# A rotary-embedding kernel: the cos and sin tables move from ScalarE's DMA queue to SyncE's

## The chip, the cores and the metric

The kernel runs on one core of one Trainium2 chip. The metric is the device time of one execution in microseconds. Before the change the median of three runs is 162.42 us (162.38 to 162.75).

## The reference

The input `x` has 16 batches of 512 positions of 1024 numbers (16 heads of 64). Each head is split into two halves of 32, and the halves are rotated by the angle of their position, whose cosine and sine stand in two tables of 512 x 32:

```python
def reference(x, cos, sin, num_heads):
    x = x.reshape(batch, seq, num_heads, head_dim)
    x1, x2 = x[..., :half_dim], x[..., half_dim:]
    cos = cos[None, :, None, :]
    sin = sin[None, :, None, :]
    return np.concatenate([x1 * cos - x2 * sin, x1 * sin + x2 * cos], axis=-1)
```

All of it is float32. 33.55 MB are read as `x` and 33.55 MB are written; the two tables have 64 KB each.

## The kernel before

**Tiles.** `x` is cut into 8 tiles of two batches. A tile has 128 partitions (2 batches x 64), and each partition holds 8 consecutive positions ("rows" below, of 1024 numbers, so 4 KB) in one piece of 32 KB. A whole tile is 4 MB. Five buffers in SBUF (`bufs`, L73) hold tiles; tiles 5, 6 and 7 use the buffers of tiles 0, 1 and 2 again.

**Loads and stores.** `load` (L78 to L80) and `store` (L82 to L84) issue DMAs on SyncE, so on SyncE's queue, in the order of the program, which the kernel fixes by hand (`manual_schedule`, L65). The first tile is loaded in four pieces, rows 0, 1, 2 to 3 and 4 to 7 (L86 and L90), the second in two, the others whole. After the loads of tiles 0 to 4 come the stores of tiles 0 to 2, the loads of tiles 5 to 7, the stores of tiles 3 and 4, and then those of tiles 5 to 7, the last in three pieces. A load into a used buffer waits for the store that emptied it, and a store waits for the compute of its tile. Each DMA counts its completion on one of eight semaphores, taken in turn in the order of the program over both queues; a DMA that takes a semaphore again waits for the one that had it before. So the whole loads of tiles 2, 3 and 4 (the ninth to eleventh DMA) wait for the first three DMAs, which are row 0 of tile 0 and the two tables.

**Tables.** The two tables go to the tile `tabs` (L87), 64 partitions of 1 KB each, by two DMAs that ScalarE issues on a queue of its own (L88 sin, L89 cos). GpSimd meanwhile builds an identity and from it a selection matrix `sel` (L95 to L104). TensorE multiplies each table by `sel` (L111), which copies the 64 partitions to 128: sin first, into the PSUM tile `pp`, then cos into `tab`. ScalarE makes from the sine a table `sns` in SBUF that has both signs (L116, L117), and a small one for two rows in PSUM, in the tile `tab`.

**Compute.** A tile's rows are worked in groups of two or three (GROUPS, L41), by a plan written out by hand for each tile (PLAN, L42). T is the product of the swapped halves with the signed sine on GpSimd (L144); B is the same on VectorE (also L144); P is the product with the cosine on VectorE, into PSUM (L147); S is the sum of the two on VectorE, back into the tile (L149). For some groups the sum goes another way: A is the cosine product in place on VectorE (L151), and M adds by two matmuls with the identity into PSUM (L156, L158), which ScalarE copies back (L159). In the first tile the plan begins with T and P of group 3, which has rows 0 and 1. So the first piece of GpSimd's work waits for rows 0 and 1 and for `sns`; the first of VectorE's waits for those rows and for the cosine in `tab`, and its second, the sum, for GpSimd's first product.

Of the kernel before, what the change touches and what calls it, by code (L numbers as in the profile page):

```python
# [12 lines left out]
def kernel(  # L13
# [8 lines left out]
    nc = tc.nc  # L22
# [32 lines left out]
    cosv = cos.rearrange("(p r) j -> p (r j)", r=R)  # L55
    sinv = sin.rearrange("(p r) j -> p (r j)", r=R)
# [21 lines left out]
    def load(t, *cuts):  # L78
        for a, b in cuts or ((0, R),):
            loads[t].append(nc.sync.dma_start(out=x_tiles[t][:, a * dim:b * dim], in_=xv[t][:, a * dim:b * dim]))  # L80
# [4 lines left out]

    load(0, (0, 1))  # L86
    tabs = fixed.tile([HP, 2, R * half], FP32, name="tabs")  # L87
    nc.scalar.dma_start(out=tabs[:, 1], in_=sinv)  # L88
    nc.scalar.dma_start(out=tabs[:, 0], in_=cosv)  # L89
    load(0, (1, 2), (2, 4), (4, 8))  # L90
    load(1, (0, 3), (3, 8))
    for t in range(2, NB):
# [5 lines left out]
        out=ident, in_=ident, compare_op=ALU.not_equal, fill=1.0,  # L98
# [5 lines left out]
                          in_=bass.AP(tensor=i64.tensor, offset=i64.offset, ap=[i64.ap[0], [0, BP], [1, HP]]))  # L104
# [117 lines left out]
```

## Time and profile before

| what | before |
|---|---|
| median of three runs | 162.42 us (162.38 to 162.75) |
| the profiled execution | 162.55 us |
| its span, first to last instruction | 160.8 us |
| VectorE (DVE) busy | 138.4 us, 86% of the span |
| GpSimd (POOL) busy | 130.3 us, 81% |
| TensorE (PE) busy | 58.5 us, 36% |
| ScalarE (ACT) busy | 14.1 us, 9% |
| moved by DMA | 67.25 MB, mean 418 GB/s over the span |

The profile is that of one execution. "Busy" counts an engine's compute instructions; instructions that only issue a DMA are not counted, and the views mark them with a q behind the engine's name (SPq for SyncE, ACTq for ScalarE). q1 is SyncE's DMA queue and q10 ScalarE's. A DMA is spread over 16 DMA engines. The share of a queue is the time that its packets took, as a share of these 16 engines' time in the stretch that is looked at. "To landing" is the time from the issue of a DMA until its completion has been counted. A packet's whole time is put down where it begins, so that shares of short stretches may be above 1.

### The profile page before, as it was taken

How to read it: one execution, taken by the hardware profiler on the slowest of the kernel's cores; microseconds unless marked ns; L12 is line 12 of the kernel's file. 1: busy time of each engine (PE TensorE's matmuls, PEld its weight loads, DVE VectorE, ACT ScalarE, POOL GpSimd, SP SyncE). 2: the span in 40 equal slices, each digit the busy share in tenths (PEclk: the TensorE clock that was granted, in tenths of full speed). 3: DMA queues.
4: the chain of work that ended last, by engine and by line, in shares of the span. 5: the costliest groups of instructions: out<-in, count | busy, mean ns of one | idle time of the engine just before them, and what ended most of it. 6: DMA issues, size and time to landing. Idle time of an engine off the chain costs nothing.

```text
span 160.8 us, 394 instructions
## 1 busy us (share of the span) xinstructions
PE 58.5 (36%) x84; PEld 18.3 (11%) x84; DVE 138.4 (86%) x48; ACT 14.1 (9%) x25; POOL 130.3 (81%) x29
## 2 busy tenths in 40 slices
PE   0500000130488803088702378896868620000000
PEld 0200000100122100032101022222222200000000
DVE  0069999999999999999999999999998999999300
ACT  3200000000011110011200011102121210000000
POOL 2299999999979299995999199999999999992000
PEclk9999999999999995557995555559999995555555
DMA  5999999999999999999999999999999999999994
GB/s 164 384 450 417 460 432 465 391 432 481 391 391 505 399 399 489 416 399 481 424 399 448 457 399 432 473 391 432 473 399 424 467 408 416 465 424 408 404 441 199
DMA packets 3329, 67.25 MB, mean 418 GB/s; under 512 B 384, under 2 KB 512, under 8 KB 768
## 3 DMA queue, kind: packets, MB, share of 16 engines
q1 hardware_dynamic: 3168, 67.11, 97.8%
q10 hardware_dynamic: 160, 0.13, 0.2%
q14 instruction: 1, 0.01, 0.0%
HBM read 33.69 MB, written 33.55 MB: 418 GB/s over the span
## 4 chain that ended last, share of the span: by engine, by line
DVE 37%; POOL 27%; DMA 18%; PE 7%; issue 2%; ACT 2%; DVEq 0%; POOLq 0%
POOL T L144 27%; DVE x_sb L149 18%; DVE pp L147 16%; DMA x_sb<-in_x_dram 16%; PE ps L158 3%; PE ps L156 3%; DMA tabs<-in_sin_dram 3%; DVE x_sb L151 1%; DVE T L144 1%; ACT x_sb L159 1%; PE pp L111 1%; ACT sns L116 0%; ACT sns L117 0%; DVEq L149 0%; POOLq L144 0%
## 5 line engine op out<-in xcount | busy, mean ns | idle before, releaser
L144 POOL TENSOR_TENSOR T<-x_sb,sns 128x3072 f32<-128x3072 f32 (+1 forms) x22 | 129.3, 5927 | 14.7 <-ACT sns L117 5.4
L147 DVE TENSOR_TENSOR pp<-x_sb,tab 128x3072 f32<-128x3072 f32 (+1 forms) x20 | 60.8, 3040 | 8.8 <-ACT tab L117 8.3
L149 DVE TENSOR_TENSOR x_sb<-T,pp 128x3072 f32<-128x3072 f32 (+1 forms) x20 | 60.7, 3033 | 2.9 <-POOL T L144 1.5
L156 PE MATMUL ps<-T,ident 128*128 128x512 f32 x40 | 30.5, 854 | 47.1 <-POOL T L144 27.7
L158 PE MATMUL ps<-x_sb,ident 128*128 128x512 f32 x40 | 28.6, 807 | 18.9 <-DVE x_sb L151 18.9
L159 ACT COPY x_sb<-ps 128x512 f32<-128x512 f32 x20 | 11.7, 586 | 110.4 <-PE ps L158 110.4
L156 PEld LDWEIGHTS ps<-T,ident 128*128 128x128 f32 x40 | 7.6, 237 | 69.8 <-POOL T L144 29.2
L158 PEld LDWEIGHTS ps<-x_sb,ident 128*128 128x128 f32 x40 | 9.7, 252 | 34.8 <-DVE x_sb L151 23.3
L151 DVE TENSOR_TENSOR x_sb<-x_sb,tab 128x2048 f32<-128x2048 f32 x5 | 11.4, 2281 | 0.0
L144 DVE TENSOR_TENSOR T<-x_sb,tab 128x2048 f32<-128x2048 f32 x3 | 6.8, 2280 | 0.0
L111 PE MATMUL pp<-tabs,sel 64*128 64x256 f32 x2 | 1.2, 697 | 5.1 <-DMA tabs<-in_sin_dram 5.1
L116 ACT ACT_TABLE_LOAD x1 | 1.3, 1283 | 1.9 <-issue 1.9
L111 PE MATMUL tab<-tabs,sel 64*128 64x256 f32 x2 | 1.2, 708 | 0.3 <-DMA tabs<-in_cos_dram 0.3
L111 PEld LDWEIGHTS pp<-tabs,sel 64*128 64x128 f32 x2 | 0.5, 310 | 5.0 <-issue 5.0
L116 ACT COPY sns<-pp 128x256 f32<-128x256 f32 x1 | 0.4, 373 | 3.1 <-PE pp L111 3.1
L111 PEld LDWEIGHTS tab<-tabs,sel 64*128 64x128 f32 x2 | 0.5, 310 | 1.0 <-DMA tabs<-in_cos_dram 1.0
L96 POOL MEMSET ident<- 128x128 f32 x1 | 0.2, 205 | 0.3 <-POOLq L203 0.3
L117 ACT ACTIVATE sns<-pp 128x256 f32<-128x256 f32 x1 | 0.4, 390 | 0.0
L97 POOL TENSOR_SCALAR_AFFINE_SELECT ident<-ident 128x128 f32<-128x128 f32 x1 | 0.3, 292 | 0.1
L103 POOL COPY sel<-ident 64x128 f32<-64x128 f32 x1 | 0.3, 283 | 0.1
L203 POOL MEMSET const-float32-0.0<- 128x1 f32 x1 | 0.1, 98 | 0.2 <-issue 0.2
L116 ACT COPY tab<-pp 128x64 f32<-128x64 f32 x1 | 0.2, 197 | 0.9 <-PE tab L111 0.9
(4 smaller groups left out, 0.5 us busy)
## 6 DMA issues: line engine op xcount, KB each, us to landing
out_dram<-x_sb SPq DMA_DIRECT2D x7, 4096.0 KB, 20.8
x_sb<-in_x_dram SPq DMA_DIRECT2D x6, 4096.0 KB, 29.1
out_dram<-x_sb SPq DMA_DIRECT2D x2, 1536.0 KB, 12.6
x_sb<-in_x_dram SPq DMA_DIRECT2D x1, 2560.0 KB, 20.4
x_sb<-in_x_dram SPq DMA_DIRECT2D x1, 2048.0 KB, 11.7
x_sb<-in_x_dram SPq DMA_DIRECT2D x1, 1536.0 KB, 14.8
x_sb<-in_x_dram SPq DMA_DIRECT2D x2, 512.0 KB, 4.5
x_sb<-in_x_dram SPq DMA_DIRECT2D x1, 1024.0 KB, 7.3
```

What stands on the lines that cost most here:

```text
L97: nc.gpsimd.affine_select(out=ident, in_=ident, compare_op=ALU.not_equal, fill=1.0, base=0, pattern=[[-1, P]], channel_multiplier=1,)
L103: nc.gpsimd.tensor_copy(out=sel.rearrange("k (b p) -> k b p", b=BP), in_=bass.AP(tensor=i64.tensor, offset=i64.offset, ap=[i64.ap[0], [0, ...
L111: spread = [nc.tensor.matmul(out=o.rearrange("p r j -> p (r j)"), lhsT=sel, rhs=tabs[:, i], start=True, stop=True) for i, o in ((1, sin_ps ...
L116: signed.append(nc.scalar.copy(out=o[:, :, 1, :], in_=sin_ps[:, r0:r0 + o.shape[1], :]))
L117: signed.append(nc.scalar.mul(out=o[:, :, 0, :], in_=sin_ps[:, r0:r0 + o.shape[1], :], mul=-1.0))
L144: return [eng.tensor_tensor(out=Ts[t, k], in0=swapped(xr, n), in1=tb, op=ALU.mult)]
L147: return [nc.vector.tensor_tensor(out=pps[t, k], in0=xr, in1=cosb(k), op=ALU.mult)]
L149: return [nc.vector.tensor_tensor(out=xr, in0=Ts[t, k], in1=pps[t, k], op=ALU.add)]
L151: return [nc.vector.tensor_tensor(out=xr, in0=xr, in1=cosb(k), op=ALU.mult)]
L156: made.append(nc.tensor.matmul(out=ps, lhsT=ident, rhs=Ts[t, k][:, c * C:(c + 1) * C], start=True, stop=False))
L158: made.append(nc.tensor.matmul(out=ps, lhsT=ident, rhs=xc, start=False, stop=True))
L159: made.append(nc.scalar.copy(out=xc, in_=ps))
```

## The change

Both table DMAs are issued by SyncE in place of ScalarE. They stand where they stood in the program: behind the load of row 0 of the first tile and ahead of that of row 1. Nothing else in the kernel's text is different.

```diff
     load(0, (0, 1))
     tabs = fixed.tile([HP, 2, R * half], FP32, name="tabs")
-    nc.scalar.dma_start(out=tabs[:, 1], in_=sinv)
-    nc.scalar.dma_start(out=tabs[:, 0], in_=cosv)
+    nc.sync.dma_start(out=tabs[:, 1], in_=sinv)
+    nc.sync.dma_start(out=tabs[:, 0], in_=cosv)
     load(0, (1, 2), (2, 4), (4, 8))
     load(1, (0, 3), (3, 8))
     for t in range(2, NB):
```

In the built kernel ScalarE's instructions begin with its table load in place of the two DMAs, and SyncE's second and third DMA are now the two tables. VectorE, GpSimd and TensorE have the same instructions in the same order; their waits name other semaphores of the same DMAs (row 0 and sin have changed places in the row of semaphores).

## Prediction

> **What bounds the kernel now.** I first read the page's slices and its DMA queues, because the busiest engine (VectorE, 86%) leaves 14% of the span open.
>
> ```profile
> DVE  0069999999999999999999999999998999999300
> ...
> DMA  5999999999999999999999999999999999999994
> ...
> q1 hardware_dynamic: 3168, 67.11, 97.8%
> q10 hardware_dynamic: 160, 0.13, 0.2%
> ```
>
> The DMA row is full from the second slice to the last but one, while VectorE's (DVE) begins a slice later and ends two slices earlier; nearly all of it is SyncE's queue, q1. I then asked for the same by stretches; the last two columns are the share of the 16 DMA engines and GB/s.
>
> ```profile
> 0.00:3.00 3.00, 0.00 (x0) 0.00 (x0) 0.00 (x0) 1.05 (x1) 0.98 (x7) 1.00 0.39 81
> 3.00:8.00 5.00, 2.40 (x4) 1.00 (x4) 0.00 (x0) 1.05 (x4) 0.96 (x1) 1.00 1.03 388
> 8.00:140.00 132.00, 56.08 (x80) 17.31 (x80) 128.54 (x45) 11.97 (x22) 122.65 (x22) 0.83 1.01 433
> 140.00:158.00 18.00, 0.00 (x0) 0.00 (x0) 9.81 (x4) 0.00 (x0) 5.66 (x1) 0.50 0.99 424
> 158.00:161.00 3.00, 0.00 (x0) 0.00 (x0) 0.00 (x0) 0.00 (x0) 0.00 (x0) 0.50 0.23 98
> ```
>
> From 3 to 158 us the DMA engines are never idle and move 66.71 MB at 430 GB/s (the DMA view of that stretch). So the time is a sum: about 3 us of start-up, 155 us of a full DMA queue, 2.8 us to the span's end, and 1.75 us outside the span (162.55 - 160.8).
>
> Has compute slack everywhere? A DMA lands when the queue reaches it, so the question is whether each store is issued before the queue has run empty. The DMA view, over the moment of each issue, gives the time to landing. The store of tile 0 is issued at 30.06 and lands 32.8 later, at 62.9; that of tile 1 is issued at 56.82, 6.0 us before. The store of tile 2 (66.12) comes 6.5 us before that of tile 1 lands (56.82 + 15.8). The last store is issued at 150.09 with 9.9 us to landing, although its 1.5 MB take only 3.7 us at 430 GB/s. Taking off some 1.7 us, the worst of what lies between the last bytes and a landing and between an issue and its first bytes, about 4 us of slack are left at the tightest place. The page's chain of waits names VectorE (37%) and GpSimd (27%) and begins with the sin table, but it ends at VectorE's last sum at 150.05: it passes over the queue in which the last store stands. I take the DMA queue as the bound, and the chain as a path with 4 us to spare.
>
> **The start, step by step.** The timeline of the first 12 us (start, duration, what, and in brackets the idle time before):
>
> ```profile
> 0.73 0.53 ACTq L88 DMA_DIRECT2D tabs<-in_sin_dram  x1
> 0.74 6.15 SPq L80 DMA_DIRECT2D x_sb<-in_x_dram  x9
> ...
> 1.30 0.62 ACTq L89 DMA_DIRECT2D tabs<-in_cos_dram  x1
> ...
> 5.07 1.19 PE L111 MATMUL pp<-tabs,sel 64*128 64x256 f32 x2 [5.07 <-DMA tabs<-in_sin_dram]
> 6.29 0.37 ACT L116 COPY sns<-pp 128x256 f32<-128x256 f32 x1 [3.07 <-PE pp L111]
> ...
> 6.58 1.22 PE L111 MATMUL tab<-tabs,sel 64*128 64x256 f32 x2 [0.33 <-DMA tabs<-in_cos_dram]
> 7.04 8.97 POOL L144 TENSOR_TENSOR T<-x_sb,sns 128x2048 f32<-128x2048 f32 x2 [5.39 <-ACT sns L117]
> ...
> 8.31 2.30 DVE L147 TENSOR_TENSOR pp<-x_sb,tab 128x2048 f32<-128x2048 f32 x1 [8.31 <-ACT tab L117]
> 11.57 2.29 DVE L149 TENSOR_TENSOR x_sb<-T,pp 128x2048 f32<-128x2048 f32 x1 [0.97 <-POOL T L144]
> ```
>
> In windows of 0.2 us SyncE's queue has its first packets from 1.7; ScalarE's has none until 3.5, though sin was issued at 0.73. In longer windows q10 has 80 packets from 3.4 to 4.2, none from 4.2 to 5.1 and 80 from 5.1 to 5.9, while q1's 80 in the middle window are 4 KB each. So the order on the DMA engines is row 0, sin, row 1, cos, rows 2 and 3: sin is already directly behind row 0, and only cos changes places with row 1. A table costs the 16 engines 24.1% of 0.8 us = 0.19 us (cos 25.4%, 0.20).
>
> (The Trainium skill, DMA: Bandwidth & Descriptors, "Queues, rings and completion order", says that each DMA engine takes turns between the queues that have work, a packet of typically 9 to 17 descriptors at a time. A DMA of 128 partitions gives each engine 8 pieces, so the order above agrees. By this rule alone the change does no more than swap cos and row 1.)
>
> **Part by part.**
> 1. *Removed from ScalarE*: two issues, 0.53 + 0.62 = 1.15 us. ScalarE's table load (1.28 us at 1.95) comes earlier, but ScalarE then waits 3 us for TensorE. Worth 0.
> 2. *Added to SyncE*: two issues between those of row 0 (0.74) and row 1 (1.17). Each is bounded by SyncE's shortest issue at L80, 0.33, and ScalarE's longer one, 0.62; I take 0.45, the middle of the steps between SyncE's first issues (0.43 to 0.59). Row 1 is issued at about 2.1 (1.8 to 2.4), and five issues behind it move by the same 0.9. Cover: row 0's issue took 1.0 us to its first packets (0.74 to 1.7), so row 1's are there at 3.1 (2.8 to 3.4). The queue works on row 0 until about 3.6 and then on two tables, 0.39, to 4.0. Cover to spare: 0.6 to 1.2. Without cover the whole 0.9 would be paid, since the DMA queue is the bound. Later loads are farther ahead: the whole load of tile 4 (SyncE's last issue of the start, at 6.56) lands 46.6 us after it. Cost 0.
> 3. *Moved on the DMA engines*: the same bytes in the same packets, in one queue. From nothing in the total: 0. Row 1, now behind cos, lands 0.2 later, at 6.5 (1.17 + 5.2 = 6.4 before). Its first reader is GpSimd at 7.04, which waited for `sns`, ready at 6.95. Cost 0, with 0.4 to spare.
> 4. *Cos earlier*: it lands about 0.2 behind sin (4.9), at 5.1 in place of 6.5. Its matmul then follows that of sin at 6.27 in place of 6.58, and VectorE's first product starts at about 8.0 in place of 8.31. Next in line is GpSimd: VectorE's sum at 11.57 waits for GpSimd's product that started at 7.04 and ends at 11.55. So the 0.3 us turn into a longer wait there (0.97 to about 1.3). Gain 0.
> 5. *Sin*: still directly behind row 0; it lands at 4.9, as before, give or take 0.1.
> 6. *Semaphore waits*: the whole loads of tiles 2, 3 and 4 wait for the same three DMAs as before (row 0, sin, cos). The last may be issued at about 5.5 in place of 6.56; it stands behind the loads before it either way. 0.
>
> Sum: 0 on the profiled 162.55, and 0 on the median; I predict **162.4**. Unknown are two ends. Below: bytes moved until 3.0 are 0.24 MB (the DMA view of 0 to 3), 0.56 us of a full queue, while 1.3 us had passed since the first packets at 1.7; at most 0.7 us are to be had from a better ramp. Above: a table that leaves the queue empty costs up to the 0.64 us by which row 0's first packets trailed its issue (end of issue about 1.1, packets at 1.7).
>
> (The same page, "Issuing engines are not separate DMA queues", says that issuing from several engines saves only the sequencer's issue time. That speaks against the change: by it SyncE gives back the 0.9 us of step 2, and the sum would be 163.3 if they were exposed. The windows above put 0.6 us and more of transfer over them, so I hold them to be hidden.)
>
> **Rivals.**
> - *Slower: small DMAs in one queue run it dry.* Place: between row 0 and row 1. If the engines fetch a queue's next DMA only when the last is nearly drained, a table that lasts 0.2 us doesn't cover the 0.64 us that a start takes, and the queue idles 0.45 us for each: 2 x 0.45 = +0.9, so 163.3. It decides from a start that takes over 0.4 us with nothing ahead. For: today two queues alternate here, so that one can prepare while the other runs; and q10's packets came 2.2 us after their issue. Against: large pieces in q1 follow each other with no gap (share 1.03 from 3 to 8 us). 16%.
> - *Faster: a quicker ramp.* Between 2.1 and 2.3 no packet starts, 0.4 us after the first ones, just when ScalarE's issues are being worked on. If they hold up row 0, the change gives 0.4 to 0.7 us, so 162.0 to 161.7. Against: the first reads after a start may need this time alone. 16%.
> - *The chain of compute decides after all.* Then the end follows GpSimd's first product. By steps 3 and 5 that moves by -0.1 to +0.1, so 162.3 to 162.5: the same forecast, by another reason. 5%.
> - That the tables don't move is excluded: SyncE's built instructions have them second and third.
>
> **Numbers.** About 0.3% (0.49 us) is what a measurement of this kernel can tell from no change: 161.9 to 162.9 is "same". Forecast 63%, rival slower 16%, rival faster 16%, chain 5%. Faster by over 0.3%: 0.11 from the ramp (some two thirds of 0.4 to 0.7 lie past 0.49) and 0.03 for parts that add up, 0.14. Slower: 0.16 of the rival and 0.02 for step 2's cover failing, 0.18. Same: 0.68. The range takes in the ramp's whole 0.7 below (161.7) and one of the two empty stretches with some more above (163.0).
>
> **What would show it.** Right: one queue, q1, with 3328 packets; no packet-free stretch between 3 and 158; cos's matmul at about 6.3, VectorE's first product at 8.0 and its wait before 11.6 grown to 1.3; GpSimd's first at 7.0. Wrong: a share well under 1 between 3.4 and 4.5, or row 1 landing after 7.0 (slower rival), row 0 landing well before 4.6 (faster rival), or the last landing moving with GpSimd's first start (chain).

## The result, and the profile after

The changed kernel is slower: a median of 164.68 us (163.70 to 165.63, six executions) against 162.58 us (162.38 to 163.11, six) for the kernel before on the same chip, a ratio of 1.0124 with a 95% interval of 1.0104 to 1.0144. The forecast was 162.4 and "no change". The profiled execution of the changed kernel took 163.70 us, the fastest of its six, with a span of 161.9; it is compared with the profiled 162.55 and 160.8 of before. So the trace shows 1.1 us of the 2.1 us between the medians.

The page of the changed kernel has the same picture as before: one full DMA row, and a VectorE row that begins later and ends earlier.

```profile
DVE  0149999999999999999999999999998999999200
...
DMA  4999999999999999999999999999999999999994
...
q1 hardware_dynamic: 3328, 67.24, 97.7%
```

All 3328 packets are in one queue, as predicted. The change did what it says, and the loss has to be found inside the full DMA row, where a tenth of a slice is 0.4 us.

**The start.** The timeline of the changed kernel, from start, duration, engine and line to the idle time before:

```profile
0.73 0.37 SPq L80 DMA_DIRECT2D x_sb<-in_x_dram  x1
...
1.17 0.53 SPq L88 DMA_DIRECT2D tabs<-in_sin_dram  x1
...
1.75 0.58 SPq L89 DMA_DIRECT2D tabs<-in_cos_dram  x1
2.37 4.29 SPq L80 DMA_DIRECT2D x_sb<-in_x_dram  x8
...
4.70 1.19 PE L111 MATMUL pp<-tabs,sel 64*128 64x256 f32 x2 [4.70 <-DMA tabs<-in_sin_dram]
...
7.34 8.97 POOL L144 TENSOR_TENSOR T<-x_sb,sns 128x2048 f32<-128x2048 f32 x2 [5.69 <-ACT tab L116]
7.54 2.30 DVE L147 TENSOR_TENSOR pp<-x_sb,tab 128x2048 f32<-128x2048 f32 x1 [7.54 <-ACT tab L117]
11.88 2.29 DVE L149 TENSOR_TENSOR x_sb<-T,pp 128x2048 f32<-128x2048 f32 x1 [2.04 <-POOL T L144]
```

Row 1, the first of the last group of loads, is issued at 2.37; before it was 1.17:

```profile
1.17 0.43 SPq L80 DMA_DIRECT2D x_sb<-in_x_dram  x1
```

Now the same moments by windows, first before, then after (the last two columns are the DMA share and GB/s):

```profile
3.50:4.00 0.50, 0.00 (x0) 0.00 (x0) 0.00 (x0) 0.00 (x0) 0.00 (x0) 1.00 1.02 387
4.00:4.50 0.50, 0.00 (x0) 0.00 (x0) 0.00 (x0) 0.00 (x0) 0.00 (x0) 1.00 1.13 375
4.50:5.00 0.50, 0.00 (x0) 0.00 (x0) 0.00 (x0) 0.00 (x0) 0.00 (x0) 1.00 0.92 360
```

```profile
3.50:4.00 0.50, 0.00 (x0) 0.00 (x0) 0.00 (x0) 0.00 (x0) 0.00 (x0) 1.00 0.85 287
4.00:4.50 0.50, 0.00 (x0) 0.00 (x0) 0.00 (x0) 0.00 (x0) 0.00 (x0) 1.00 0.97 135
4.50:5.00 0.50, 0.30 (x1) 0.33 (x2) 0.00 (x0) 0.00 (x0) 0.00 (x0) 1.00 0.66 158
5.00:5.50 0.50, 0.50 (x2) 0.17 (x1) 0.00 (x0) 0.00 (x0) 0.00 (x0) 1.00 0.90 356
```

From 4.0 to 5.0 the rate is less than half. The share falls much less (0.97 and 0.66), which is the trap in this view: engines had a packet open that took far longer than its bytes need. The trace's packet records show the packet that straddles this gap taking 0.4 to 1.0 us on most engines; packets of the same size, 1 KB and 4 KB, take 0.046 and 0.159 us at other times. Some of the slow packets are those of cos, the others those of row 1. So read GB/s, not the share. From 3 to 8 us before moved 1.94 MB, after 1.68; the difference is 0.60 us of a full queue at 432 GB/s. Part is made good later: at 30 us the changed kernel's bytes are 0.46 us behind.

The gap also leaves the 16 engines ragged. Before, they end row 1 within 0.4 us of each other, after within 1.2 to 1.4 us (in its two profiles), and a DMA has landed only when its slowest engine is done. The last part of tile 1's load lands at 3.19 + 20.4 = 23.6 before and at 4.42 + 20.0 = 24.4 after (issue plus time to landing): 0.8 us later. By the completion records the landings of tiles 2 and 3 are 0.8 us later too, so what the slowest engine lost at the start isn't made good.

**The turn from loads to stores.** A second loss lies far from the start. Here is the DMA view of 48 to 54 us, where the queue passes from the load of tile 4 to the store of tile 0: before, then after, then a second profile of the changed kernel.

```profile
DMA packets 95, 2.59 MB, mean 431 GB/s; under 512 B 16, under 2 KB 16, under 8 KB 16
```

```profile
DMA packets 84, 2.23 MB, mean 371 GB/s; under 512 B 16, under 2 KB 16, under 8 KB 16
```

```profile
DMA packets 72, 2.00 MB, mean 333 GB/s; under 512 B 11, under 2 KB 11, under 8 KB 11
```

The changed kernel lacks (431 - 371) x 6 / 432 = 0.83 us of transfer here, and 1.36 us the second time. The packet records show where: in the first profile 27 packets of 32 KB that start between 49.3 and 52.4 take 1.3 to 2.0 us in place of 1.22, in the second 31 take up to 2.5. Before, two do, both 1.6 us and on one engine. A DMA lands by its slowest engine, so the kernel before pays for those two as well, and the difference in the landings is smaller than that in the bytes: by the completion records the load of tile 4 lands at 53.15 before and at 54.26 after, 1.1 us later. The last store lands 1.15 us later: 0.8 from the start, 0.3 from the turn. In the second profile tile 4 lands at 54.86, 1.7 us later than before: 0.75 from the start and 0.95 from the turn.

### The profile page after: what moved, and what is told of

Same layout as the page of the kernel before. It is cut to its first block, busy times and chain, and to the rows that moved or that the text cites. A ratio compares the mean times of both kernels' runs of the same rounds, so it can differ in the third digit from the quotient of the medians.

```text
span 161.9 us, 394 instructions
## 1 busy us (share of the span) xinstructions
PE 61.1 (38%) x84; PEld 18.7 (12%) x84; DVE 138.4 (85%) x48; ACT 14.1 (9%) x25; POOL 130.2 (80%) x29
## 3 DMA queue, kind: packets, MB, share of 16 engines
q1 hardware_dynamic: 3328, 67.24, 97.7%
## 4 chain that ended last, share of the span: by engine, by line
DVE 36%; POOL 27%; DMA 18%; PE 8%; issue 2%; ACT 1%; SPq 0%; DVEq 0%; POOLq 0%
POOL T L144 27%; DVE x_sb L149 17%; DMA x_sb<-in_x_dram 16%; DVE pp L147 16%; PE ps L158 3%; PE ps L156 3%; DMA tabs<-in_sin_dram 2%; DVE x_sb L151 1%; DVE T L144 1%; ACT x_sb L159 1%; PE pp L111 1%; PE tab L111 1%; SPq L80 0%; ACT tab L116 0%; DVEq L149 0%
## 5 line engine op out<-in xcount | busy, mean ns | idle before, releaser
L156 PE MATMUL ps<-T,ident 128*128 128x512 f32 x40 | 31.7, 886 | 44.2 <-POOL T L144 28.7
L158 PE MATMUL ps<-x_sb,ident 128*128 128x512 f32 x40 | 29.9, 839 | 18.9 <-DVE x_sb L151 18.9
```

What stands on the lines that cost most here:

```text
L156: made.append(nc.tensor.matmul(out=ps, lhsT=ident, rhs=Ts[t, k][:, c * C:(c + 1) * C], start=True, stop=False))
L158: made.append(nc.tensor.matmul(out=ps, lhsT=ident, rhs=xc, start=False, stop=True))
```

## The experiments

**Theory** (A in the expectations): row 1 is issued too late, and the queue has run out before its data flow. **Rivals:** small DMAs in SyncE's queue run it dry wherever they stand (B, the slower rival of the prediction); the chain of compute decides (C). The table collects all runs. "Behind" is the bytes moved by 30 us against before, in us at 432 GB/s; "T" is the shift of GpSimd's first product; "turns" is the time by which packets of 8 KB and more took longer than their kind usually does, summed and divided by 16, around the turns of the queue at 36 to 56, 72 to 88 and 100 to 116 us. These three columns are worked out from the records of the one profiled execution; "turns" is a mean over the engines, so one slow engine hardly shows in it.

| kernel | row 1 issued | behind | T | turns | profiled | ratio (95%) |
|---|---|---|---|---|---|---|
| before | 1.17 | 0 | 0 | 0.07 | 162.55 | |
| before_again | 1.17 | 0.00 | -0.05 | 0.08 | 162.86 | 0.9991 (0.9978-1.0004) |
| changed | 2.37 | 0.46 | 0.30 | 0.80 | 163.70 | 1.0124 (1.0104-1.0144) |
| after_again | 2.36 | 0.29 | 0.17 | 1.15 | 164.05 | 1.0089 (1.0064-1.0113) |
| late_row1_2 | 2.71 | 0.23 | -0.19 | 0.94 | 163.93 | 1.0097 (1.0063-1.0131) |
| late_row1_1 | 1.71 | 0.53 | 0.06 | 0.01 | 163.03 | 1.0046 (1.0024-1.0067) |
| sin_sp | 1.74 | 0.21 | 0.44 | 0.73 | 164.06 | 1.0058 (1.0044-1.0073) |
| cos_sp | 1.74 | 0.70 | 0.96 | 0.00 | 163.21 | 1.0052 (1.0032-1.0072) |
| behind_row1 | 1.16 | -0.09 | 1.24 | 1.27 | 164.82 | 1.0034 (1.0000-1.0069) |
| row1_act | 0.74, ScalarE | -0.10 | 1.14 | 0.62 | 162.68 | 1.0032 (1.0006-1.0058) |
| two_rows_first | with row 0 | -0.25 | 1.15 | 0.39 | 162.52 | 1.0035 (1.0018-1.0053) |
| two_rows_act | with row 0 | -0.29 | 1.16 | 1.46 | 164.52 | 1.0109 (1.0065-1.0152) |
| turn_after | as changed | 0.31 | -0.06 | 1.19 | 164.13 | 1.0092 (1.0061-1.0123) |
| turn_before | as before | 0.03 | 0.05 | 0.10 | 162.61 | 1.0034 (1.0015-1.0054) |
| late_store0 | as changed | 0.33 | 0.25 | 1.09 | 164.27 | 1.0139 (1.0106-1.0171) |
| late_compute | 1.17 | 0.00 | 1.11 | 1.34 | 164.03 | 1.0025 (1.0007-1.0042) |
| late_all | moved by 0.5 | 0.51 | 0.51 | 0.04 | 162.84 | 1.0031 (1.0015-1.0047) |
| late_tabs | 1.17 | -0.14 | 3.88 | 1.77 | 164.45 | 1.0156 (1.0125-1.0188) |

**The two kernels once more.** `after_again` and `before_again` are the changed kernel and the kernel before, unedited.

> The changed kernel, unedited, for a second profile and the spread. The one profile of it was its fastest execution (163.70 against a median of 164.68). All theories: about 164.7 again, +1.2% on before. Theory A (SyncE's queue runs dry between the tables and row 1, and the DMA engine that loses most sets the end): an execution of 164.7 shows the DMA engines' moments of finishing row 1 spread over more than the 1.2 us of that profile, and its last landing later by the same amount. Theory B (small DMAs in SyncE's queue cost wherever they stand) and theory C (the end follows GpSimd's first product, which began 0.3 later): C expects GpSimd's first product 2 us later than before in such an execution, about 9.0.

> The kernel before, unedited, for a second profile. The first shows, besides the start, a stretch near 50 us (the end of tile 4's load, where the queue turns to stores) in which two packets of one DMA engine were slow, while after the change those of nearly all 16 were. If this second loss goes with the ragged start, this profile shows 0 to 0.1 us of it per engine again; if it is a matter of chance, it may show as much as after (0.8).

The loss is there again (164.26 us, 1.0089), and the kernel before compared with itself gives 0.9991. The bound of 0.3% holds.

**Row 1 late, tables left on ScalarE.** `late_row1_2` is the kernel before with two fillings of row 1's place, 0.98 us each, that its load must wait for. `late_row1_1` has one.

```diff
     nc.scalar.dma_start(out=tabs[:, 0], in_=cosv)
+    for c in (1, 1):
+        nc.gpsimd.memset(bufs[0][:, dim:2 * dim], 0.0)
     load(0, (1, 2), (2, 4), (4, 8))
```

> The tables stay on ScalarE as before; GpSimd clears the place of row 1 twice, and SyncE's load of row 1 waits for that, so that it and all behind it are issued at about 2.5 in place of 1.17 (2.37 after the change). A: the queue runs dry as after the change, although no table is in it: 163.6 to 165. B: no table in SyncE's queue, so as before, 162.4 to 162.7. C: row 1 lands about 0.8 later, GpSimd's first product begins at about 7.4, +0.3: 162.7 to 162.9.

> As the run with row 1 held back by two clearings (which gave +1.0%), but with one clearing, so that row 1 is issued at about 1.7 in place of 2.7; tables on ScalarE. A (the queue runs dry when row 1 is issued too late): row 0 and the two tables keep the engines until about 4.0; the lateness of first data after an issue seen so far is 1.4 to 2.3 us, so row 1 issued at 1.7 is just in time: 162.4 to 163.2, clearly under the two clearings. If the loss came from any wait on SyncE ahead of row 1, and not from its length: 163.6 to 164.2 again.

`late_row1_2` took 163.99 us, 1.0097: a loss of the size of the change's (1.0124 and 1.0089), with no table in SyncE's queue. Its timeline has row 1 at 2.71, and its windows the same dip:

```profile
2.71 0.33 SPq L80 DMA_DIRECT2D x_sb<-in_x_dram  x1
```

```profile
4.00:5.00 1.00, 0.12 (x1) 0.15 (x1) 0.00 (x0) 0.00 (x0) 0.00 (x0) 1.00 0.82 193
```

GpSimd's first product starts at 6.84, 0.2 us earlier than before, and still the kernel is 1% slower: the chain of compute is not what costs the time. In the profile of `late_row1_2` 0.4 us of the loss lie at the start (tile 1's load lands at 24.0), 0.4 at the first turn, and the rest behind 120 us.

With row 1 at 1.71 (`late_row1_1`, 163.38 us) about half is lost. It was expected to be just in time, and isn't; its dip is shallower:

```profile
4.00:5.00 1.00, 0.01 (x1) 0.04 (x1) 0.00 (x0) 0.00 (x0) 0.00 (x0) 1.00 0.97 274
```

**One table each.** `sin_sp` and `cos_sp` move one of the two lines of the change. Row 1 is then issued at 1.74.

```diff
-    nc.scalar.dma_start(out=tabs[:, 1], in_=sinv)
+    nc.sync.dma_start(out=tabs[:, 1], in_=sinv)
```

> Half of the change: sin on SyncE behind row 0, cos left on ScalarE. Row 1 is then issued at about 1.75 in place of 1.17 (before) and 2.37 (after). A: just in time, 162.4 to 163.2, less than half of the change's loss. B (each small DMA in SyncE's queue costs its share wherever it stands): half of the change's loss, 163.3 to 163.8.

> The other half of the change: cos on SyncE behind row 0, sin left on ScalarE; row 1 is issued at about 1.75. With sin alone on SyncE the same lateness gave +0.6%. A: again part of the loss, 163.2 to 164.0. B: half of the change's loss, 163.3 to 163.8; this run tells little between them, but the two halves and the whole together say whether the loss grows by steps with each table or with the moment of row 1.

163.79 and 163.57 us, 1.0058 and 1.0052: about the same half as one filling, whichever table it is. The first lies in the range of B and above that of A, the second in both, so these two runs alone don't speak against B. Nor do the profiles show a start that grows worse with the lateness of row 1: "behind" is 0.21 to 0.70 with row 1 at 1.7 and 0.23 to 0.46 at 2.4 to 2.7. It is the medians that grow.

**Tables on SyncE, but x ahead of them.** `behind_row1` puts them behind row 1; `row1_act` has the changed order, with row 1 issued by ScalarE at 0.74; `two_rows_first` loads rows 0 and 1 as one DMA ahead of them. The diffs, in this order, are against the changed kernel; all three have the last load line of the first.

```diff
+    load(0, (1, 2))
     nc.sync.dma_start(out=tabs[:, 1], in_=sinv)
     nc.sync.dma_start(out=tabs[:, 0], in_=cosv)
-    load(0, (1, 2), (2, 4), (4, 8))
+    load(0, (2, 4), (4, 8))
```

```diff
     nc.sync.dma_start(out=tabs[:, 0], in_=cosv)
+    loads[0].append(nc.scalar.dma_start(out=x_tiles[0][:, dim:2 * dim], in_=xv[0][:, dim:2 * dim]))
```

```diff
-    load(0, (0, 1))
+    load(0, (0, 2))
```

> Both tables stay on SyncE, but behind row 1 in place of ahead of it. A: row 1 is issued at 1.17 as before and the queue always has 1 us or more of x ahead of the tables and of rows 2 and 3, so it doesn't run dry: 162.4 to 162.9, within 0.3% of before. B: the same two small DMAs in the same queue, so as after, 164.2 to 164.9. C: sin lands about 1 us later than before, GpSimd's first product begins about 1 us later, so 163.4 to 164.

> The tables stay on SyncE as after the change, but row 1 is issued by ScalarE on its own queue at about 0.75, so that SyncE's issues of the tables no longer stand ahead of it. A: the engines have row 1 to work on when row 0 is done, and rows 2 and 3 (issued at 2.4 by SyncE) have the cover of row 1 and the tables: 162.4 to 162.9. B: the two small DMAs are in SyncE's queue as after: 164.2 to 164.9.

> As after the change, but the first load has rows 0 and 1 in one DMA (1 MB), then the two tables on SyncE, then rows 2 and 3. A: the first load covers the issue of the tables and of the next rows with 2.4 us in place of 1.2, so the queue doesn't run dry: 162.2 to 162.9. B: two small DMAs in SyncE's queue as after, 164.2 to 164.9. C: sin lands about 1 us later, +1: 163.4 to 164.

162.82, 163.16 and 163.30 us, 1.003 in all three. The dip is gone; this is `behind_row1`, where before had 368 GB/s:

```profile
4.00:5.00 1.00, 0.00 (x0) 0.00 (x0) 0.00 (x0) 0.00 (x0) 0.00 (x0) 1.00 1.06 417
```

With the same two small DMAs in the same queue, the queue starts at least as well as before. So small DMAs don't run it dry by themselves: what counts is what stands behind them and when. But these kernels aren't back at 1.000, and the last two lie above the ranges of A. Of `behind_row1`'s 12 executions eight took 162.5 to 162.9 us and four 164.8 to 165.0; the profiled one is of the four, and loses 1.27 us at the turns. Moving the tables behind more of x makes GpSimd's first product 1.1 to 1.2 us later.

**Rows 0 and 1 as one DMA, tables on ScalarE.** `two_rows_act`:

```diff
-    load(0, (0, 1))
+    load(0, (0, 2))
...
-    load(0, (1, 2), (2, 4), (4, 8))
+    load(0, (2, 8))
```

> The kernel before with the first tile loaded in two pieces, rows 0 and 1 and then rows 2 to 7, in place of four; tables on ScalarE. A: SyncE has two issues fewer, the queue has more ahead of it and larger packets; the start of the run with two rows first was 0.25 us ahead of before at 15 us, so 162.2 to 162.7, between 0.3 us faster and the same. C: sin lands about 1 us later, +1: 163.5.

164.74 us, 1.0109, with the best start of all. But cos, on ScalarE's queue, landed only at 10.8, 9.5 us after its issue: it took turns with the 3 MB that SyncE's queue had open. By the packet records each DMA engine moved one of cos's pieces of 1 KB between two of 24 KB of rows 2 to 7, about 1.0 us apart, from 5.9 to 10.3. VectorE's first sum came 3.4 us later. Against the intention this became a test of late compute.

**Where the turn's loss comes from.** `turn_after` and `turn_before` take the load of tile 4 from its place and issue it behind the store of tile 0, in the changed kernel and in that of before.

```diff
-    for t in range(2, NB):
+    for t in range(2, NB - 1):
         load(t)
...
             store(t)
+        if t == 0:
+            load(NB - 1)
```

> The changed kernel with the load of tile 4 moved behind the store of tile 0, so that the queue turns from loads to stores at about 43 us and back at about 53, in place of one turn at 53. It is for the second loss, 0.4 to 1.2 us near 50 in nearly all profiles but those of before. If it belongs to a turn between loads and stores, the slow packets move to about 40 to 44 (and perhaps 50 to 54); if it belongs to tile 4's data, to 59 to 63; if to the time since the start, they stay at 48 to 53 although stores run there. Time 163.7 to 166.

> The same move in the kernel before. If the kernel before has no second loss because its engines are in step, this one has none either at the new turns: 162.4 to 162.9. If before only happens to escape it by the place of its turns, this one may show it: 163.2 and more.

In `turn_after` the first change from load to store comes one tile earlier, and the loss goes with it: of 1.19 us at the turns nearly all lies around 40 us. The DMA view of 40 to 44 us, before and then `turn_after`:

```profile
DMA packets 69, 1.74 MB, mean 434 GB/s; under 512 B 16, under 2 KB 16, under 8 KB 16
```

```profile
DMA packets 48, 1.25 MB, mean 311 GB/s; under 512 B 10, under 2 KB 10, under 8 KB 10
```

So it goes with the turn, and not with the moment or with tile 4's load. `turn_before` has a turn at the same place and no such loss in its profile, though it is 0.3% slower than before over ten executions.

`late_store0` is the changed kernel with the store of tile 0 held back, by a copy of one column on VectorE in the work of tile 2, so that it is issued at 49.47 in place of 30.36.

```diff
+    def late():
+        nc.vector.tensor_copy(out=bufs[0][:, 0:1], in_=bufs[0][:, 0:1])
+        store(0)
```

> The changed kernel with the store of tile 0 issued at about 49.2 us in place of 30.4 (it waits for a copy of one column of its own tile onto itself, which VectorE makes in tile 2's work); the last packets of tile 4's load end at 52.6 to 53.9. If the slow packets at the turn come of the store being read ahead, they begin only after about 50.3 and are fewer (under 0.5 us per engine in place of 0.8 to 1.2): 163.3 to 164. If they don't depend on the store being there, they begin at 49.4 as before and the loss is the same: 164 to 165.

164.83 us, 1.0139. In its profile the turn near 50 us lost 0.12 in place of 0.75, and the slow packets began 1.1 us after the store's issue. This is what was expected if the waiting store is the cause, but `late_row1_1` and `cos_sp` had no loss at this turn with the store in its usual place, so one profile can't show it. The time lies in the range of the other answer: the next turns lost 0.97, and nothing was gained.

**Compute and queue, each moved alone.** `late_compute` is the kernel before with the filling of the identity repeated: every product 1.1 us later, no DMA of the start touched. `late_all` delays row 0 and both tables by 0.5 us, by fillings of their places, so that queue and compute shift together. `late_tabs` holds back the tables alone.

```diff
-    nc.gpsimd.memset(ident, 0.0)
+    for c in range(18):
+        nc.gpsimd.memset(ident, 0.0)
```

```diff
-    load(0, (0, 1))
     tabs = fixed.tile([HP, 2, R * half], FP32, name="tabs")
+    nc.gpsimd.memset(bufs[0][:, 0:512], 0.0)
+    nc.gpsimd.memset(tabs[:, 1, 0:16], 0.0)
+    load(0, (0, 1))
```

```diff
     tabs = fixed.tile([HP, 2, R * half], FP32, name="tabs")
+    for c in range(2):
+        nc.gpsimd.memset(tabs.rearrange("p s f -> p (s f)"), 0.0)
```

> The kernel before, with GpSimd clearing the identity 18 times in place of once, so that sel is ready at about 5.5 to 5.9 in place of 1.65, and the first product of GpSimd begins about 0.5 to 0.9 later; loads and tables are issued exactly as before. If slow packets at a turn come of the compute's place against the queue, part of the executions lie at 163.3 and more and the profile has 0.3 us or more of them. If the queue's own start sets them, all executions lie at 162.3 to 163.2, with 0.1 us of them in the profile.

> The kernel before, with the load of row 0 and the tables' DMAs both held back by about 0.5 us (GpSimd clears half of row 0 and a little of the tables first), so that the queue and the compute begin later together. Every theory: the queue's start moves by 0.5, +0.5 us, 163.0 to 163.4. If the distance between compute and queue matters alone, no slow packets at the turns (0.1 us); if any change of the start brings them, 0.3 us and more, and executions of 164 and above.

> The kernel before, with both tables still on ScalarE, but issued about 1 us later (GpSimd clears their place twice, and their DMAs wait for it), so that sin comes behind row 1 and lands at about 6, like in the run with the tables behind row 1 on SyncE. Start-up of x as before, compute about 1.2 us later. If the slower executions of that run (164.8 to 165.0, 4 of 12) come of the later compute, this run has them too: a part of the executions at 164 and more. If they come of tables in SyncE's queue, all lie between 162.3 and 163.3. By the prediction's 4 us of slack: 162.3 to 162.9.

`late_all`: 163.22 us, 0.5 more for a queue that is 0.5 us late. In the medians a delay of the whole queue goes to the end at its full size; in the one profile (162.84) 0.3 us of it are left at the end, and hardly a packet at a turn is slow. `late_compute`: 163.02 us, 1.0025. Its bytes at 30 us are those of before, and most of its 12 executions took 162.6 to 163.3. The profiled one, 164.03, has slow packets at the later turns, as the DMA view of 104 to 114 us shows; before, and then `late_compute`:

```profile
DMA packets 151, 4.42 MB, mean 442 GB/s; under 512 B 16, under 2 KB 16, under 8 KB 16
```

```profile
DMA packets 139, 4.03 MB, mean 403 GB/s; under 512 B 16, under 2 KB 16, under 8 KB 16
```

That is (442 - 403) x 10 / 432 = 0.9 us. So the turns can cost time with an undisturbed start as well. `late_tabs` made VectorE's sums 4.85 us later, more than was meant: the store of tile 2 is issued at 70.97, 0.9 us before that of tile 1 lands (59.63 + 12.3 = 71.9), too late to follow it without a gap. 164.81 us, 1.0156: the slack of compute is used up.

None of these kernels is faster than the kernel before.

## Why the prediction was wrong

- **The bound: right.** The DMA queue sets the time. `late_all` pays for its delay in full (by the medians), and `late_row1_2` is slower with compute that is earlier. The slack of 4 us agrees with `late_tabs`, where 4.85 us used it up, but it did not mean that smaller shifts are free: 1.1 us cost 0.25% in `late_compute`.
- **Step 1 (ScalarE): right.** Its table load came earlier and nothing waited for it.
- **Step 2 (SyncE): this failed, in its cover.** The size of the issues was at the range's upper end: 0.53 and 0.58 us where I took 0.45, so row 1 at 2.37 (range 1.8 to 2.4). The cover was counted with row 0's *first packets*, 1.0 us after issue. Those first packets are not the full rate: row 0 was issued at 0.74, and the rate is still 195 GB/s (before) and 174 (after) from 2.4 to 2.8, and 427 and 408 only from 2.8 to 3.5. That is 2.0 us. Row 1 took still longer, 2.37 to 5.0. With the prediction's own 4.0 for the end of row 0 and the tables the cover was 4.0 - (2.37 + 2.0) = -0.4 us and not +0.6 to +1.2. Cos, issued at 1.75, was late in the same way: part of the slow packets are its own. But 2.0 us is no fixed price: by it row 1 at 1.71 would have had 0.3 us to spare, and `late_row1_1` has a dip too (303, 246 and 303 GB/s in the half microseconds from 3.5 to 5.0). What sets this time the runs don't show. The slow ramp stood in the prediction's own windows, and I priced it only as a gain that might be had.
- **Step 3 (row 1's landing): direction right, size wrong.** It landed at 7.17, not at 6.5. So GpSimd's first product, at 7.34, waits for row 1, which cost 0.3 us there and not 0; `sns` was ready at 6.58. (The view names ScalarE's copy into `tab`, which ended at 7.27. Before, the same product started at 7.04, ahead of that copy, which began at 7.84, so it isn't what the product needs.)
- **Step 4 (cos): right in what came of it.** Cos landed at 5.8, and not at 5.1, but in time for its matmul at 5.82, where 6.27 was forecast. VectorE's first product came earlier (7.54; 8.0 was forecast) and the gain went into the wait behind it, 2.04 us in place of 0.97 (1.3 was forecast; GpSimd's product is 0.3 us later).
- **Step 5 (sin): nearly right.** Sin landed at 4.6, not at 4.9, and its matmul started at 4.70 in place of 5.07.
- **Step 6 (waits): right.** The load of tile 4 was issued at 6.12 (5.5 was forecast), 48 us before its landing.
- **The slower rival** had the place, its sign (row 1 landed after 7.0) and, at 163.3, most of the profiled loss, but a wrong cause. It made the tables' own start the price, 0.45 us each; `behind_row1` has the same tables in the same queue and no dip, and `late_row1_2` has the dip without them.
- **Not seen at all: the turn.** The profiles of the changed kernel lose 0.8 and 1.15 us per engine in slow packets where loads turn to stores; both profiles of before lose less than 0.1. The sum had no term for it.

(The Trainium skill, DMA: Bandwidth & Descriptors, "Issuing engines are not separate DMA queues", says that more issuing engines save only the sequencer's issue time. The sum by it was 163.3. The trace agrees with the sense of it: two issues, 1.11 us, stood ahead of a load that the queue needed at once. They delayed it by 1.2 us, and the landings by 0.8.)

**What stays open.** What decides whether packets at a turn are slow was not found. They came with a late row 1 (`late_row1_2`, `sin_sp`) and without one (`late_compute`, `behind_row1`), and a late row 1 came without them (`late_row1_1`, `cos_sp`). That the engines' raggedness after the start provokes them at the first turn is only argued. So of the 1.24%, about 0.5% can be put down to the late start (0.8 us in the landings of both profiles of the changed kernel, and the loss of the two kernels whose profiles have a late start alone, `late_row1_1` and `cos_sp`), and the turns account for the rest of the two profiled executions; the slower ones, up to 165.63 us, were not profiled. That the rest follows from the late row 1 too is shown only as a whole, by `late_row1_2`, and not step by step.

## What to carry to other kernels

Where the DMA queue is the bound, its first DMAs have to be issued so that the next large one is at full rate when the last runs out; here that took 2.0 us and more from the issue, and row 1 at 1.71, some 2.3 us before row 0 and the tables ran out, was still too late. So look for the full rate in GB/s, not for the first packet and not for the DMA share. Two small DMAs ahead of the second load cost 0.9 to 1.2% here, and behind a second large load 0.3%. On another engine's queue they stand in no load's way, but one can land late beside large pieces, as cos did in `two_rows_act`. A slack that was found at the end of a chain tells when the chain becomes the bound, and not that shifts below it are free.

## What the runs showed of the hardware

- Where row 1 was issued 1.2 us later, single packets of 1 and 4 KB took 0.4 to 1.0 us in place of 0.046 and 0.159, and the 16 engines came out of it up to 1.4 us apart, where they were 0.4 apart before. That the queue had run out is read from the rate; no record shows it directly.
- At a turn from loads to stores in one queue, packets of 32 KB took 1.3 to 2.5 us in place of 1.22, in some profiles and not in others: up to 1.46 us per engine over all turns (`two_rows_act`; `late_tabs` has 1.77, with a store issued too late among it), 0.07 in the kernel before.
- Two queues took turns piece by piece in `two_rows_act`: one of 1 KB, one of 24 KB, so that a DMA of 64 KB landed 9.5 us after its issue.
- An issue on SyncE took 0.37 us for row 0's 128 partitions of 4 KB, and 0.53 and 0.58 us for a table's 64 partitions of 1 KB: a DMA of an eighth of the bytes had the longer issue.
